# The last group of an experts' stage in a written order, its halves summed in the same banks; the embedding gate's start by token tiles

## The chip, the cores and the metric

The kernel runs on one core of a Trainium2 chip. The metric is the time of one execution in device microseconds (us). A core has a matmul engine (TensorE, PE in the profile, with its weight loads shown apart as PEld), VectorE (DVE), ScalarE (ACT), GpSimd (POOL), and a queue engine (SP), which issues nearly all of this kernel's transfers. Matmul results go to PSUM, a memory of eight banks; here they are two pools of four, "a" and "b".

## The reference

256 tokens of 1024 numbers (h) go through two layers and then a third block. Each layer is attention, then experts, then a gated embedding; the part that matters here, from the reference and cut:

```
h = h + mix                                                # attention
h = h + hier_moe(rms_norm(h, ln_ffn[i]), ...)              # experts
gate = jax.nn.sigmoid(rms_norm(h, ln_ple[i]) @ ple_w_gate[i])
h = h + gate * (p[i] @ ple_w_proj[i])                      # embedding gate

# hier_moe: 4 groups of 8 experts, each 1024 -> 128 -> 1024; a token takes one group and 2 experts of it
hid = silu(einsum('td,edf->tef', xt, w_gate)) * einsum('td,edf->tef', xt, w_up)
y = einsum('tef,efd->td', hid * cw[:, :, None], w_down)    # cw: weight of each token and expert
```

After the second layer comes a block with conditioning: a feed-forward part, a mixer, a second feed-forward part and a last norm, each preceded by a norm that is scaled and shifted. All is float32.

## The kernel before

**Layout.** h lies on chip as [128, 2, 1024]: two tiles of 128 tokens (t = 0, 1) by 1024 columns, cut into 8 pieces of 128 (kk, or k) and two halves of 512 (n, or ci). A float32 product is made of three faster ones: each operand is split into a high part, written by ACT, and a low part (the operand less its high part), written by DVE; mm3 then issues high x high (L306), high x low (L307) and low x high (L308). For weights this split is halves(): L293 on ACT, L294 on DVE, for a transfer of 1 MB in two parts (tiles raw to hi and lo).

**The experts' stage.** Function moe(i) runs once in each layer. For each of four groups (gq) tokens are gathered into slots, 32 for an expert, so that half a group (pp, four experts) fills 128 rows. A half goes through these steps:
- gate_up (L1056), four units u of two k each: the gathered tokens of an expert by its gate and up weights, plain float32; four experts lie side by side in 32 columns each of PE.
- the hidden tile, in finish(): Tanh on ACT (L1085), two steps on DVE (L1086, L1087), a transpose on PE (L1089), a copy on ACT (L1091).
- the down products (L1096): for each of the two column halves, four products of 32 columns side by side, one for each expert, into one bank of pool "a". One such group of four is called a set below. ACT scales the bank and writes its high part (L1099), DVE its low part (L1100), in tiles of the pool w4.
- token parts: two transposes (L1079) and a copy (GT, L1081) give the matrix that brings slots back to tokens.
- combine(): sums (L1109) of GT by high and low part into a bank, for each t and n, then an add on DVE to h (L486).

For groups 0 to 2, combine() sums both halves of a group in one bank and adds once. For the last group it runs for each half alone: finish(3, 0), combine, finish(3, 1), combine, each with four banks, eight sums and four adds. The down weights (wd) take their slots from the pools of hi and lo, four each.

**The embedding gate.** ple(i) follows. gained_T transposes h on PE (L373), 16 pieces of 128x128, and evacuates them by kk, both token tiles together (128x256): high part on ACT (L378), low part on DVE (L379). Then dense() multiplies by the gate's weights in two column parts of 512 (ci), 96 products in each; for the first part every weight piece is used for both token tiles at once, for the last part tile 0 runs through all weights and then tile 1. put() finishes each with Tanh, an embedding product that was made earlier, and an add to h (L1409 to L1411). The stage that follows begins with a norm's scale (rstd), the transposes of h by token tile (L419 transposes the scale) and, in the third block, modulated_T (L424 to L426).

**What sets the order.** Each engine runs its instructions in a fixed order that a scheduler works out when the kernel is built: each instruction has a priority by its place in the program, moved ahead by a fixed amount inside `with self.ahead_by(...)` (300 for "finish", 200 for "gain", 60 for "split"), and is placed when its operands and a free buffer are there by the scheduler's own estimate. Buffers go round in pools: raw 9, e 7, w4 5, hi and lo 4 each, GT 2, PSUM 4 and 4. DMAs are issued on SP as the raw tiles come free.

## Time and profile before

| what | us |
|---|---|
| median of 3 runs (1118.27 to 1119.1) | 1118.55 |
| the profiled execution | 1120.68 |
| its span in the trace | 1118.9 |
| end of the experts' stage, first layer | 289.16 to 324.64 |
| end of the experts' stage, second layer | 549.70 to 585.19 |
| gate of the second layer | 585.19 to 608.50 |
| start of the third block, to its first product | 608.50 to 617.04 |

The mean granted clock of TensorE over the profiled execution is 0.985. The profile is of one execution, about 2 us longer than the runs' median. Its numbers are of instructions on each engine: busy time, the mean duration of one, and the idle time before an instruction with what released it. Lines are those of the kernel before.

### The profile page before, as it was taken

What the parts mean: (1) busy time and instruction counts of PE and PEld (TensorE: products, weight loads), DVE (VectorE), ACT (ScalarE), POOL (GpSimd) and SP (SyncE); (2) the same over time, 40 slices, a digit from 0 to 9 for tenths busy, and PEclk for the clock granted to TensorE, in tenths of its full rate; (3) what the DMA queues carried; (4) which work ended last, traced back from release to release, by engine and by line L of the source; (5) the groups of instructions that cost most, each with busy time, mean ns of one, the idle gap of its engine ahead of it and who ended that gap; (6) DMA issues with size and microseconds to landing.
All of it is one profiled execution on the core that took longest, in us unless ns stands there. A gap on an engine that the chain in (4) does not pass through costs nothing.

```text
span 1118.9 us, 18106 instructions
## 1 busy us (share of the span) xinstructions
PE 1066.2 (95%) x6957; PEld 821.9 (73%) x6957; DVE 698.3 (62%) x1720; ACT 518.9 (46%) x1009; POOL 37.8 (3%) x43
## 2 busy tenths in 40 slices
PE   7999999999989999999989999999989989999996
PEld 6885557765547758666537799899969768999995
DVE  6686785644368965644358756575684866554555
ACT  5445585322257675222236544434454645444442
POOL 3000000200100000300000000000000000000000
PEclk9998999899999999999999999999999999999998
DMA  9656657599984477699795655845675354454310
GB/s 375 277 216 266 255 217 291 184 370 389 415 338 157 182 283 289 231 373 388 274 374 194 264 186 215 309 172 180 219 305 189 113 199 178 177 185 165 131 41 37
DMA packets 46506, 268.53 MB, mean 240 GB/s; under 512 B 5328, under 2 KB 7120, under 8 KB 20432
## 3 DMA queue, kind: packets, MB, share of 16 engines
q1 hardware_dynamic: 46416, 267.34, 63.4%
q8 instruction: 56, 0.92, 0.3%
q14 instruction: 34, 0.28, 0.1%
HBM read 266.27 MB, written 1.05 MB: 239 GB/s over the span
## 4 chain that ended last, share of the span: by engine, by line
PE 47%; DVE 3%; ACT 1%; issue 1%; DVEq 0%; ACTq 0%
PE b L306 7%; PE b L307 7%; PE b L308 7%; PE a L306 6%; PE a L308 6%; PE a L307 6%; PE a L1056 1%; DVE lo L294 1%; PE a L1096 1%; PE a L1450 1%; PE a L1109 1%; PE b L1466 1%; DVE w L1488 1%; DVE h L1489 0%; PE b L1035 0%
## 5 line engine op out<-in xcount | busy, mean ns | idle before, releaser
L294 DVE TENSOR_TENSOR lo<-raw,hi 128x1024 fp32r<-128x1024 f32 (+2 forms) x234 | 271.5, 1164 | 187.6 <-ACT hi L293 186.7
L293 ACT ACTIVATE hi<-raw 128x1024 fp32r<-128x1024 f32 (+2 forms) x234 | 234.6, 1008 | 247.5 <-PE b L307 125.5
L306 PE MATMUL a<-hi,e 128*128 128x512 f32 (+2 forms) x576 | 225.3, 392 | 1.8 <-ACT e L378 1.8
L307 PE MATMUL a<-lo,e 128*128 128x512 f32 (+2 forms) x576 | 223.7, 389 | 0.0
L308 PE MATMUL a<-hi,e 128*128 128x512 f32 (+2 forms) x576 | 222.8, 389 | 0.0
L306 PE MATMUL b<-e,hi 128*128 128x256 f32 x640 | 181.8, 284 | 0.0
L307 PE MATMUL b<-e,hi 128*128 128x256 f32 x640 | 181.4, 283 | 0.0
L308 PE MATMUL b<-e,lo 128*128 128x256 f32 x640 | 181.3, 283 | 0.0
L306 PEld LDWEIGHTS a<-hi,e 128*128 128x128 f32 x576 | 109.1, 190 | 25.0 <-ACT e L378 2.9
L308 PEld LDWEIGHTS a<-hi,e 128*128 128x128 f32 x576 | 108.8, 189 | 22.9 <-DVE e L379 1.1
L307 PEld LDWEIGHTS a<-lo,e 128*128 128x128 f32 x576 | 109.2, 190 | 21.5 <-DVE lo L294 1.2
L306 PEld LDWEIGHTS b<-e,hi 128*128 128x128 f32 x640 | 123.0, 192 | 1.1 <-ACT hi L293 0.8
L307 PEld LDWEIGHTS b<-e,hi 128*128 128x128 f32 x640 | 123.0, 192 | 0.3
L308 PEld LDWEIGHTS b<-e,lo 128*128 128x128 f32 x640 | 122.9, 192 | 0.0
L1056 PE MATMUL a<-raw,e 128*32 128x256 f32 x832 | 73.5, 383 | 1.1 <-DVEq L1293 0.8
L581 ACT ACTIVATE p<-p,m 128x128 f32<-128x128 f32 (+1 forms) x96 | 42.6, 448 | 8.9 <-DVE m L576 6.6
L486 DVE TENSOR_TENSOR h<-h,a 128x512 f32<-128x512 f32 x48 | 31.9, 685 | 21.7 <-PE a L1109 14.4
L1056 PEld LDWEIGHTS a<-raw,e 128*32 128x32 f32 x832 | 31.6, 110 | 18.6 <-issue 2.1
L1099 ACT ACTIVATE w<-a,sv 128x512 fp32r<-128x512 f32 x32 | 21.6, 687 | 46.6 <-PE a L1096 41.6
L1096 PE MATMUL a<-wd,hT 128*32 128x512 f32 x256 | 42.4, 600 | 0.0
L1035 PE MATMUL b<-G,e 128*128 128x256 f32 x256 | 38.9, 298 | 3.3 <-DVE ssv L351 2.0
L1109 PE MATMUL a<-w,GT 128*128 128x512 f32 x128 | 35.8, 412 | 6.2 <-ACT w L1099 5.1
(316 smaller groups left out, 1375.9 us busy)
## 6 DMA issues: line engine op xcount, KB each, us to landing
raw<-in_ffn SPq DMA_DIRECT2D x62, 1024.0 KB, 4.8
raw<-in_moe_gu SPq DMA_DIRECT2D x52, 1024.0 KB, 8.3
raw<-in_w_ada SPq DMA_DIRECT2D x36, 1024.0 KB, 5.1
wd<-in_moe_dn SPq DMA_DIRECT2D x64, 512.0 KB, 6.7
raw<-in_w_gate SPq DMA_DIRECT2D x8, 1024.0 KB, 11.2
raw<-in_w_m_in SPq DMA_DIRECT2D x8, 1024.0 KB, 4.9
raw<-in_w_a_in SPq DMA_DIRECT2D x7, 1024.0 KB, 10.9
e<-in_moe_gu SPq DMA_DIRECT2D x6, 1024.0 KB, 9.8
```

Of the source, the lines that this page charges most:

```text
L293: nc.scalar.activation(hi[:, sl], raw[:, at], AF.Copy)
L294: eng.tensor_tensor(lo[:, sl], raw[:, at], hi[:, sl], op=OP.subtract)
L306: mm(out, l[0], r[0], start=start, stop=False, **kw)
L307: mm(out, l[0], r[1], start=False, stop=False, **kw)
L308: mm(out, l[1], r[0], start=False, stop=stop, **kw)
L486: self.nc.vector.tensor_tensor(self.h[:, t, sl], self.h[:, t, sl], ps, op=OP.add)
L581: nc.scalar.activation(p, p, AF.Exp, bias=m[:, i:i + 1], scale=-1.0, accum_out=den[:, i:i + 1])
L1035: nc.tensor.matmul(ps[:, j], xh[part][:, t, sl], G[:, t], start=(t + j + part == 0), stop=(t + part == 2), skip_group_check=True)
L1056: nc.tensor.matmul(pgs[pp][32 * x:32 * x + 32], xg[:, k, o:o + 32], wg[kk][:, x], start=(k == 0), stop=(k == KT - 1))
L1096: nc.tensor.matmul(py[32 * x:32 * x + 32], hT[:, 32 * x:32 * x + 32], wd[2 * n + x // 2][:, x % 2], start=True, stop=True)
L1099: nc.scalar.activation(yh[:, sl], py, AF.Identity, scale=cw)
L1109: nc.tensor.matmul(ps, GT[:, t * P:(t + 1) * P], y[:, n * 512:(n + 1) * 512], start=(b == 0), stop=(b == len(back) - 1))
```

## The change

The last group of each experts' stage gets a function of its own, last_group(), whose instructions keep the order in which they are written (inline() stamps them on a line "tail" that the scheduler must follow). Group 2's combine moves into it. In it:
- both sets of a half are issued one after the other into pool "b", and only then their high and low parts are made (down_products);
- the sums of both halves of the last group go to the same four banks of pool "a" (start with the first product of the first half, stop with the last of the second), and h is added to once for each t and n, in the order of t;
- the token parts of both halves come after group 2's sums;
- the last group's second gate/up product takes its bank from pool "b";
- the split of the gate's first weight tile is called before the second hidden tile (gate_first, handed to dense()).

In K the head of ple goes from 0 to 1: gained_T evacuates by token tile (128x128 pieces, 16 on each engine, moved ahead by 200), and the first column part of the gate's products runs tile by tile too. The diff, cut to these parts:

```diff
-    head={'nsa': 0, 'ple': 0, 'moba': 0, 'mixer': 1},
+    head={'nsa': 0, 'ple': 1, 'moba': 0, 'mixer': 1},
...
+    def inline(self, ins, line="tail"):
+        self.tc.stamp_issue_order_token(ins.ins, line)
+        return ins
...
+        def down_products(gq, pp, wd, hT):
+            cw = st[gq][4][0][:, pp, 1:2]
+            with self.ahead_by("finish"):
+                yh, yl = self.w4([P, D], F32R), self.w4([P, D], F32R)
+                pys = []
+                for n in range(2):
+                    py = self.psb([P, 512])
+                    pys.append(py)
+                    for x in range(4):
+                        inline(nc.tensor.matmul(py[32 * x:32 * x + 32], hT[:, 32 * x:32 * x + 32],
+                                                wd[2 * n + x // 2][:, x % 2], start=True, stop=True))
+                for n, py in enumerate(pys):
+                    sl = slice(n * 512, (n + 1) * 512)
+                    inline(nc.scalar.activation(yh[:, sl], py, AF.Identity, scale=cw))
+                    inline(nc.vector.scalar_tensor_tensor(yl[:, sl], py, cw, yh[:, sl], op0=OP.mult, op1=OP.subtract))
+            return yh, yl
...
+        def last_group(back, values):
+            list(values)
+            first_hidden = hidden(3, 0)
+            next(first_hidden)
+            gate_up(3, 1, 0, None, self.psb)
+            gate_up(3, 1, 1)
+            hT = next(first_hidden)
+            combine_half(back, 0)
+            gate_up(3, 1, 2)
+            combine_half(back, 1)
+            GT = [token_parts(pp) for pp in range(2)]
+            gate_up(3, 1, 3)
+            y = [down_products(3, 0, wd[3, 0], hT)]
+            self.fine = bool(K["fine"])
+            self.gate_first = [list(self.halves(self.unit("w_gate", i * D * D, 2048), 2048, 4))]
+            second_hidden = hidden(3, 1)
+            next(second_hidden)
+            acc = [[self.psa([P, 512]) for _ in range(2)] for _ in range(2)]
+
+            def gathered(pp, n, t):
+                for part in range(2):
+                    inline(nc.tensor.matmul(acc[t][n], GT[pp][:, t * P:(t + 1) * P], y[pp][part][:, n * 512:(n + 1) * 512],
+                                            start=(pp + part == 0), stop=(pp + part == 2)))
+
+            with self.ahead_by("finish"):
+                for n in range(2):
+                    gathered(0, n, 0)
+                hT = next(second_hidden)
+                for n in range(2):
+                    gathered(0, n, 1)
+                y.append(down_products(3, 1, wd[3, 1], hT))
+                for t in range(2):
+                    for n in range(2):
+                        gathered(1, n, t)
+                        inline(self.add_h(n, t, acc[t][n]))
...
+            if gq == 3:
+                last_group(back, values)
+                break
...
+            if gq == 2:
+                continue
             combine(back)
```

hidden(), token_parts() and combine_half() hold the same instructions as finish() and combine() did, each stamped. In the order of the changed kernel the lines are others: gate_up L1062, hidden tile L1130 to L1138, down products L1151, parts L1155 and L1156, sums of the last group L1189, adds L492, splits L299 and L300.

The first place is PE near the end of the second layer's experts' stage: down products (w.. and hT to a bank), sums (GT) and, in the new order, the second hidden tile's transpose (hb). Before:

```order
L1096 MATMUL a_5993<-wd_5826,hT_5982 32x512 x2
L1109 MATMUL a_6000<-w4_5984,GT_5974 128x512
L1109 MATMUL a_6000<-w4_5985,GT_5974 128x512
L1109 MATMUL a_6004<-w4_5984,GT_5974 128x512
L1109 MATMUL a_6004<-w4_5985,GT_5974 128x512
L1096 MATMUL a_5993<-wd_5828,hT_5982 32x512 x2
L1109 MATMUL a_6008<-w4_5984,GT_5974 128x512
L1109 MATMUL a_6012<-w4_5984,GT_5974 128x512
L1096 MATMUL a_6031<-wd_5892,hT_6027 32x512 x2
L1109 MATMUL a_6008<-w4_5985,GT_5974 128x512
L1109 MATMUL a_6012<-w4_5985,GT_5974 128x512
L1096 MATMUL a_6031<-wd_5894,hT_6027 32x512 x2
```

And in the new order:

```order
L1136 MATMUL b_6037<-consts_88,hb_6025 128x128
L1189 MATMUL a_6031<-w4_5997,GT_5982 128x512
L1189 MATMUL a_6031<-w4_5998,GT_5982 128x512
L1189 MATMUL a_6032<-w4_5997,GT_5982 128x512
L1189 MATMUL a_6032<-w4_5998,GT_5982 128x512
L1151 MATMUL b_6047<-wd_5900,hT_6039 32x512 x2
L1151 MATMUL b_6047<-wd_5902,hT_6039 32x512 x2
L1151 MATMUL b_6052<-wd_5904,hT_6039 32x512 x2
L1151 MATMUL b_6052<-wd_5906,hT_6039 32x512 x2
L1189 MATMUL a_6029<-w4_6045,GT_5987 128x512
L1189 MATMUL a_6029<-w4_6046,GT_5987 128x512
L1189 MATMUL a_6030<-w4_6045,GT_5987 128x512
```

Before, the sets of a half come in pairs with sums between them, and the second half's sums have banks of their own; now the eight down products of a half stand together, and its sums go on in the banks of the first half (a_6029 to a_6032).

The second place is DVE from the last low part of the experts' stage into the gate (h the adds, e the gate's operands, raw its weights). Before:

```order
L1100 SCALAR_TENSOR_TENSOR w4_6030<-a_6038,sv_5951,w4_6029 128x512
L486 TENSOR_TENSOR h_87<-h_87,a_6053 128x512
L486 TENSOR_TENSOR h_87<-h_87,a_6057 128x512
L379 SCALAR_TENSOR_TENSOR e_6062<-b_6063,small_89,e_6061 128x256
L379 SCALAR_TENSOR_TENSOR e_6062<-b_6064,small_89,e_6061 128x256
L294 TENSOR_TENSOR lo_6131<-raw_6128,hi_6130 128x512 x2
L294 TENSOR_TENSOR lo_6149<-raw_6128,hi_6148 128x1024
L351 SCALAR_TENSOR_TENSOR ssv_6108<-ss_6099 128x2
```

And in the new order:

```order
L1156 SCALAR_TENSOR_TENSOR w4_6046<-b_6052,sv_5917,w4_6045 128x512
L492 TENSOR_TENSOR h_87<-h_87,a_6029 128x512
L492 TENSOR_TENSOR h_87<-h_87,a_6030 128x512
L492 TENSOR_TENSOR h_87<-h_87,a_6031 128x512
L492 TENSOR_TENSOR h_87<-h_87,a_6032 128x512
L396 SCALAR_TENSOR_TENSOR e_6074<-b_6075,small_89,e_6073 128x128
L396 SCALAR_TENSOR_TENSOR e_6074<-b_6076,small_89,e_6073 128x128
L300 TENSOR_TENSOR lo_6016<-raw_6013,hi_6015 128x512
```

All four adds now follow the last low part, where before two of them did; the evacuations are of 128x128 (sixteen in all, where eight of 128x256 stood; an order row stands for equal rows in a run), and the first weight split follows them.

The third place is DVE at the end of the second layer's gate and the start of the third block (raw_6446 and raw_6462 the feed-forward part's weights, w4 and h the gate's last steps, ssv the norm's scale). Before:

```order
L1410 SCALAR_TENSOR_TENSOR w4_6287<-w4_6287,e_4784 128x512
L1411 TENSOR_TENSOR h_87<-h_87,w4_6287 128x512
L294 TENSOR_TENSOR lo_6449<-raw_6446,hi_6448 128x1024
L420 COPY rbc_6311<-a_6310 128x128
L294 TENSOR_TENSOR lo_6459<-raw_6446,hi_6458 128x1024
L351 SCALAR_TENSOR_TENSOR ssv_6354<-squares_6202 128x1
L424 SCALAR_TENSOR_TENSOR xn_6322<-b_6308,mods_704,rbc_6311 128x128
L316 TENSOR_SCALAR nh_6357<-ssv_6354 128x1
```

And in the new order:

```order
L300 TENSOR_TENSOR lo_6465<-raw_6462,hi_6464 128x1024
L1511 SCALAR_TENSOR_TENSOR w4_6303<-w4_6303,e_4792 128x512
L300 TENSOR_TENSOR lo_6475<-raw_6462,hi_6474 128x1024
L1512 TENSOR_TENSOR h_87<-h_87,w4_6303 128x512
L300 TENSOR_TENSOR lo_6487<-raw_6484,hi_6486 128x1024
L426 COPY rbc_6327<-a_6326 128x128
L357 SCALAR_TENSOR_TENSOR ssv_6370<-squares_6194 128x1
L300 TENSOR_TENSOR lo_6497<-raw_6484,hi_6496 128x1024
L322 TENSOR_SCALAR nh_6373<-ssv_6370 128x1
```

A large weight split (128x1024) now stands between the gate's last two steps on DVE, where before they stood together. The orders on SP and POOL are the same in both kernels.

## Rows read from the trace of the kernel before

**Rows 1.** The page's first part: busy us (share of the span) and instructions.
```profile
PE 1066.2 (95%) x6957; PEld 821.9 (73%) x6957; DVE 698.3 (62%) x1720; ACT 518.9 (46%) x1009; POOL 37.8 (3%) x43
```

**Rows 2.** Windows: stretch, length, busy PE PEld DVE ACT POOL, clock, DMA, GB/s.
```profile
289.16:324.64 35.48, 30.67 (x239) 14.56 (x239) 15.62 (x31) 9.97 (x25) 1.89 (x2) 1.00 1.01 415
549.70:585.19 35.49, 30.68 (x240) 14.55 (x239) 15.63 (x31) 9.97 (x25) 0.00 (x0) 1.00 0.96 377
584.46:608.50 24.04, 23.50 (x102) 18.29 (x101) 19.22 (x45) 14.98 (x28) 0.00 (x0) 1.00 0.55 194
608.50:617.04 8.54, 5.79 (x52) 2.78 (x50) 7.59 (x23) 6.36 (x11) 0.00 (x0) 1.00 0.61 216
```

**Rows 3.** Chain of waits, second tail: start, length, engine, line and count.
```profile
568.75 1.01 PE a L1096 x8
569.78 0.69 ACT w L1099
570.50 0.76 DVE w L1100
...
572.27 1.01 PE a L1096 x4
```

**Rows 4.** PE's waits, 556.3 to 585.3: waiter, releaser, us in all, count, longest.
```profile
PE a L1109 <- ACT w L1099: 2.5, 4, 0.8
```

**Rows 5.** Timeline of PE and DVE, second tail: start, length, engine, line, operation.
```profile
547.12 1.93 PE L1096 MATMUL a<-wd,hT 128*32 128x512 f32 x16
...
556.39 1.05 PE L1096 MATMUL a<-wd,hT 128*32 128x512 f32 x4
...
560.15 3.49 PE L1109 MATMUL a<-w,GT 128*128 128x512 f32 x14
...
563.57 3.66 PE L1056 MATMUL a<-raw,e 128*32 128x256 f32 x64
...
583.17 1.28 DVE L486 TENSOR_TENSOR h<-h,a 128x512 f32<-128x512 f32 x2 [0.71 <-PE a L1109]
```

**Rows 6.** A window in the second gate.
```profile
598.00:608.00 10.00, 10.00 (x46) 8.29 (x45) 6.58 (x16) 4.25 (x9) 0.00 (x0) 1.00 0.51 188
```

**Rows 7.** Groups by form, 549.7 to 637.5: count, busy us, mean ns, idle before.
```profile
L425 ACT ACTIVATE e<-xn,mods 128x128 fp32r<-128x128 f32 x16 | 5.6, 391 | 4.9 <-DVE xn L424 4.9
L426 DVE SCALAR_TENSOR_TENSOR e<-xn,mods,e 128x128 fp32r<-128x128 f32 x16 | 5.2, 349 | 0.2 <-ACT e L425 0.2
...
L379 DVE SCALAR_TENSOR_TENSOR e<-b,small,e 128x256 fp32r<-128x256 f32 x8 | 3.7, 479 | 0.0
...
L1091 ACT ACTIVATE hT<-b 128x128 f32<-128x128 f32 x3 | 0.8, 268 | 0.0
...
L1087 DVE SCALAR_TENSOR_TENSOR hb<-hb,rr,a 128x128 f32<-128x128 f32 x2 | 0.7, 348 | 0.1
...
L1089 PE MATMUL b<-consts,hb 128*128 128x128 f32 x2 | 0.7, 328 | 1.1 <-DVE hb L1087 1.1
```

**Rows 8.** Timeline of DVE, second gate and the third block's start.
```profile
589.83 1.22 DVE L294 TENSOR_TENSOR lo<-raw,hi 128x1024 fp32r<-128x1024 f32 x1
...
618.10 0.93 DVE L426 SCALAR_TENSOR_TENSOR e<-xn,mods,e 128x128 fp32r<-128x128 f32 x3
```

**Rows 9.** DMA issues, 560.0 to 560.7 and 562.4 to 563.0: KB, us to landing.
```profile
raw<-in_w_gate SPq DMA_DIRECT2D x1, 1024.0 KB, 6.0
...
raw<-in_w_gate SPq DMA_DIRECT2D x1, 1024.0 KB, 12.8
```

**Rows 10.** PE's waits, 608.5 to 640.
```profile
PE a L419 <- DVE rstd L325: 2.8, 1, 2.8
```

**Rows 11.** Windows around the third block's start.
```profile
613.20:617.00 3.80, 1.05 (x11) 0.84 (x10) 3.80 (x18) 2.23 (x5) 0.00 (x0) 1.00 0.98 382
618.60:621.90 3.30, 3.30 (x9) 2.60 (x8) 3.30 (x9) 1.05 (x4) 0.00 (x0) 0.52 1.00 420
621.90:625.00 3.10, 3.10 (x15) 2.54 (x14) 1.23 (x5) 1.16 (x4) 0.00 (x0) 1.00 1.02 431
```

More of the change, by code (lines that the diff above doesn't have):

```diff
@@ L1045, in gather, with gate_up @@
                 gather_tile(gq, k, ps, t)
-        def gate_up(gq, pp, u, beside=None):
+        def gate_up(gq, pp, u, beside=None, bank=None):
             _, _, xg, pgs, _ = st[gq]
             if u == 0:
-                pgs.append(self.psa([P, 2, P]))
+                pgs.append((bank or self.psa)([P, 2, P]))
             where, wg = ahead.pop((gq, pp, u))
@@ L1055, in gate_up @@
                     o = pp * P + 32 * x
[L1056 to L1057 removed]
+                    mm = nc.tensor.matmul(pgs[pp][32 * x:32 * x + 32], xg[:, k, o:o + 32], wg[kk][:, x],
+                                          start=(k == 0), stop=(k == KT - 1))
+                    if gq == 3 and pp:
+                        inline(mm)
                     if beside and x % K["svx"] == 0:
@@ L1101, in finish, with token_parts @@
             return [(GT, yh), (GT, yl)]
+        inline = lambda ins: self.inline(ins, f"tail{i}")
+        def token_parts(pp):
+            G = st[3][0]
+            pv = self.psb([P, T])
+            for t in range(2):
+                inline(nc.tensor.transpose(pv[:, t * P:(t + 1) * P], G[:, t, pp * P:(pp + 1) * P].bitcast(F32),
+                                           self.ident))
+            GT = self.wk.tile([P, T], F32R, tag="GT", name="GT")
+            inline(nc.scalar.activation(GT, pv, AF.Copy))
+            return GT
@@ new lines, in hidden @@
+        def hidden(gq, pp):
+            pgs, (_, rr) = st[gq][3:]
+            pg = pgs[pp]
+            with self.ahead_by("finish"):
+                hb = self.wk.tile([P, P], F32, tag="hb", name="hb", bufs=1)
+                inline(nc.scalar.activation(hb, pg[:, 0], AF.Tanh, scale=rr[:, 0, pp:pp + 1]))
+                inline(nc.vector.scalar_tensor_tensor(hb, hb, 1.0, pg[:, 0], op0=OP.add, op1=OP.mult))
+                inline(nc.vector.scalar_tensor_tensor(hb, hb, rr[:, 1, pp:pp + 1], pg[:, 1], op0=OP.mult, op1=OP.mult))
+            yield
+            with self.ahead_by("finish"):
+                pt = self.psb([P, P])
+                inline(nc.tensor.transpose(pt, hb, self.ident))
+                hT = self.wk.tile([P, P], F32, tag="hT", name="hT", bufs=1)
+                inline(nc.scalar.activation(hT, pt, AF.Copy))
+            yield hT
@@ new lines, in down_products @@
+        def down_products(gq, pp, wd, hT):
+            cw = st[gq][4][0][:, pp, 1:2]
+            with self.ahead_by("finish"):
+                yh, yl = self.w4([P, D], F32R), self.w4([P, D], F32R)
[11 more added lines that the diff above has]
+            return yh, yl
@@ new lines, in combine_half @@
+        def combine_half(back, n):
+            for t in range(2):
+                ps = self.psa([P, 512])
+                for b, (GT, y) in enumerate(back):
+                    inline(nc.tensor.matmul(ps, GT[:, t * P:(t + 1) * P], y[:, n * 512:(n + 1) * 512],
+                                            start=(b == 0), stop=(b == len(back) - 1)))
+                inline(self.add_h(n, t, ps))
+        def last_group(back, values):
[20 more added lines that the diff above has]
+                                            start=(pp + part == 0), stop=(pp + part == 2)))
+            with self.ahead_by("finish"):
+                for n in range(2):
[4 more added lines that the diff above has]
+                y.append(down_products(3, 1, wd[3, 1], hT))
+                for t in range(2):
+                    for n in range(2):
+                        gathered(1, n, t)
+                        inline(self.add_h(n, t, acc[t][n]))
@@ L1225, in moe @@
             point(gq, 1)
-            if gq < 3:
-                slots_start(gq + 1)
-                slots(gq + 1)
-                for k in range(4):
-                    gather(gq + 1, k)
-            back = finish(gq, 0, wd[gq, 0])
-            if gq == 3:
-                combine(back)
-                back = []
-            else:
-                if not hold:
-                    load_down(gq + 1, 0)
-                for u in range(4):
-                    gate_up(gq + 1, 0, u)
+            slots_start(gq + 1)
+            slots(gq + 1)
+            for k in range(4):
+                gather(gq + 1, k)
+            back = finish(gq, 0, wd[gq, 0])
+            if not hold:
+                load_down(gq + 1, 0)
+            for u in range(4):
+                gate_up(gq + 1, 0, u)
             back = back + finish(gq, 1, wd[gq, 1])
             point(gq, 2)
-            if gq < 3 and not hold:
+            if not hold:
                 load_down(gq + 1, 1)
             point(gq, 3)
+            if gq == 2:
+                continue
             combine(back)
@@ L1413, in put @@
                 self.square_new(ci, t)
-        self.fine = bool(K["fine"])
-        self.dense(x, "w_gate", [512, 512], put, off=i * D * D, tail=True, head=K["head"]["ple"])
+        self.dense(x, "w_gate", [512, 512], put, off=i * D * D, tail=True, head=K["head"]["ple"], first=self.gate_first)
     def ada_start(self):
```

5 lines of the change are left out of this document (2 added, 3 removed).

## The prediction

> **What bounds the kernel now.** The page's first part comes first: PE is busy for 95% of the span [rows 1], so only time in which PE waits, or works in a slow form, can be won. Then the windows by stage: each experts' stage ends in a stretch of 35.5 us, from the first gate/up product of the last group to the first product of the embedding gate, in which PE is busy for only 30.7 us, at the full clock. The two stages agree to 0.01 us, so what is worked out for the second holds for the first too [rows 2]. The chain of waits in that stretch shows a round trip that comes back for every half of the down products: a set of products on PE, its high part on ACT (0.69 us), its low part on DVE (0.76), and only then the sums on PE [rows 3]. PE's own waits name the same place: 2.5 us in 4 waits for ACT's high part [rows 4]. There is also a loss that no wait shows. Four down products of 32 columns each run side by side: 16 records (8 products) take 1.93 us, so a set of four costs about 0.88 from start to start [rows 5]. Before issues several of them in pairs with other work between, and a pair (4 records) takes 1.01 us in the chain, like a whole set (8 records) [rows 3]. From 556.39 on the order has eight such slots where five sets would do: three too many.
>
> **The tail, step by step.** I start where both orders are alike, at the last set of group 2. Before is there at 556.39 [rows 5]; the two token transposes ahead of it (0.2 us) now come later, so 556.2. Durations [rows 5]: a set 0.88; eight sums 1.9 (14 span 3.49); a gate/up unit 0.87 (four span 3.66, of which 0.2 overlaps what follows); a change from 128-column to 32-column work 0.24 (563.57 less 560.15 less 14 x 0.227); an add 0.60 from start to start (two span 1.28). A product of the gate takes 0.227: 46 records touch 10 us, two of them in part [rows 6].
> - The set ends at 557.1. Two gate/up units (1.74) cover the hidden tile's steps on ACT and DVE, which are through at 558.2 as before; with its transpose, 559.0.
> - Eight sums, a change, a unit, eight sums, four token transposes (0.4), a change, a unit: 1.9 + 0.24 + 0.87 + 1.9 + 0.4 + 0.24 + 0.87 = 6.4, to 565.4. ACT and DVE have over 2 us for group 2's remaining parts, and its adds lie beside this.
> - Two whole sets: readable at 566.45 and 567.35. ACT 0.69 each, DVE 0.75 each: low parts at 567.95 and 568.85. The second hidden tile stands behind them on both engines: its Tanh (0.37) lies beside, then two steps of at most 0.35 on DVE, to 569.5 [rows 7].
> - Transpose 0.33 and copy 0.27 [rows 7]: 570.15. Beside it PE does the first half's sums, the last four after the transpose, to 570.6; a change: 570.8.
> - Two sets: readable at 571.85 and 572.75. ACT to 573.45, DVE to 574.2. The added wait is here: all four adds stand behind both low parts on DVE, and the transposes of h behind the adds. 3 x 0.60 + 0.68: h is whole at 576.7.
>
> Before has h whole at 584.45, the end of the two adds at 583.17 [rows 5]. The tail gives back 7.75 us.
>
> **The gate.** Before needs 24.05 us from there to the last product's end [rows 2]. In the new order DVE has, after the last add, sixteen evacuations of 128x128, two small and three large low parts. That evacuation does not stand in the gate before; the nearest rows are those of its size at the next stage's start, 0.39 on ACT and 0.35 on DVE for one [rows 7], and three on DVE span 0.93, so 0.28 or 0.29 each in a row [rows 8]. 16 x 0.28 + 2 x 0.60 + 2 x 1.17 + 1.22 = 9.3: the first two units' last low part is ready at about 586, against 591.05 before [rows 8]. Behind it the order has 64 of the 96 products, 14.5 us: the end is 600.7, again 24.0 us after h is whole. So I take the gate at no gain and no loss. DVE's extra 2.7 us (9.3 less 6.6) is hidden because 32 products are issued ahead of that split, where before had 19 (77 fit behind 591.05). Without that cover the gate costs up to 2.7 us more per stage. The early split of the first unit brings nothing: on ACT it stands behind the last high part.
>
> The rows show DVE at 0.48 us for one evacuation of 256 and 0.35 for one of 128 [rows 7]. The Trainium skill (Perfetto Trace Analysis, Optimizing Scalar/DVE Operations) says that each operation carries a fixed access cost, so that grouping helps a saturated engine, while smaller pieces may let work finish sooner where the engine is not saturated but holds up others. By its first half the gain would be 5.4 us smaller, by its second the sum stands. Which half applies no row settles: DVE is busy for 19.2 of the gate's 24.0 us [rows 2].
>
> **The rest.** Transfers: the order on SP is unchanged. The gate's weights land 6.0 us after the first issue at about 560.6 and 12.8 us after the last at about 562.5, so by 575.3 [rows 9]. They stand behind group 2's last down weights, whose slot now comes free some 3 us earlier, so I expect the last by about 572. The first is needed at 575.5, the second at 580: nothing is lost; without that cover each us late is a us lost.
> The next stage's start changes in the second stage only: PE waits there 2.8 us for the second half's scale [rows 10]. On DVE one large low part now stands between the last gate product's two steps, and the evacuations' first steps stand among the scale's chain. Stepped through, the first product starts 9.3 us after the gate's end instead of 8.54 [rows 2]: plus 0.8, with bounds of 0 (the chain waits for the square anyway) and 2.0.
> Other bounds, over both stages: sets that do not overlap (1.05 instead of 0.88, eight of them) plus 1.4; evacuations at 0.39 instead of 0.28 plus 3.5; the gate without cover plus 5.4; from below, a gate whose early products leave no stall (96 x 0.227 = 21.8 from 576.5, so 2.4 less each) minus 4.8. I take the values in the sum, those of the nearest rows.
>
> **Sum.** 2 x 7.75 = 15.5 off, 0.8 on: 14.7 us off. Against the profiled execution's own 1120.68 us (span 1118.9) that is 1106.0. The median of the runs, 1118.55, lies 2.1 lower, so I predict 1103.9 us. All later work only starts sooner.
>
> **Rivals.**
> - The gate loses what DVE has more. For: the last low part, not PE, sets when the dense run begins. Against: 32 products are there to fill. Plus 5.4 to 6 us: 1109.6.
> - A larger gain, the gate without a stall: for, PE can start it at 576.5; against, DVE's 9.3 us. 1099.
> - Slower: the clock falls in the new tail. At a granted 0.52, the lower level (1.2 GHz), PE did 9 products in 3.3 us, and 15 in 3.1 at the upper one; it had fallen after 3.8 us in which PE was busy for 1.05 [rows 11]. Between 565.4 and 586 the new order has 48 products and four sets with pauses between; at the lower level they cost 48 x 0.20 + 4 x 0.88 = 13.1 us more per stage. This decides once more than 7.4 of the 13.1 are lost, that is with the clock low for over half of that stretch; low throughout it is 1118.55 - 14.7 + 26.2 = 1130. Against: before has pauses of the same kind in its tail, at 1.00 throughout [rows 2].
> - It does not do what it says: the gate's products of both token tiles stand interleaved, not tile by tile; if the sums wait for banks as well, nothing is won: 1118.
> The Trainium skill (Perfetto Trace Analysis, Matmuls) wants independent groups to rotate through the banks, so that one is read beside the next group's products. Here four banks are held until the last half is in, and the adds stand bare, 2.5 us instead of 1.3; that is in the steps above already.
>
> **Numbers.** The forecast (1101 to 1107) 0.58; the smaller gain (1107 to 1116) 0.24; the larger 0.10; no change 0.03; slower 0.05. The range 1099 to 1111.5 leaves out the last two and the far ends of the second and third, under 2 in 10. A change of 0.2% (2.2 us) is about the least that can be told from none here. Faster 0.92, same 0.03, slower 0.05.
>
> **What would show it.** Right: the stretch to the first gate product near 27 us instead of 35.5 in both stages; the last group's down products in four slots; four adds in a row right before the transposes of h; the gate's end 23 to 25 us after the last add; clock 1.00. Wrong: PE waiting for a PSUM bank or a down weight in the tail, a gate of 27 us, a granted clock near 0.5 before the dense run, or a next stage that starts over 10.5 us after the gate.

## The result

The changed kernel takes 1105.86 us (median of 4, 1103.13 to 1108.57) against 1118.82 before; the ratio is 0.9878, with a 95% interval of 0.985 to 0.9906. Forecast were 1103.9 us and a range of 1099 to 1111.5. Timed once more beside the first experiments it is 1105.21 (6 runs) against 1119.36, ratio 0.9868 [0.9848, 0.9888].

Its ten executions lie in two groups, 1102.2 to 1103.4 and 1107.1 to 1108.6, and the mean granted clock goes with them: 0.988 to 0.990 in the first, 0.983 to 0.985 in the second. So kernels are compared below in two ways that do not hang on this: by the length of a stage in the trace, and by the span times its mean granted clock, an estimate of the span at the full clock. (It takes half of all time at the lower level away, also where PE had to wait anyway.) This span times clock is 1103.1 before (mean of 11 runs) and 1088.2 after (10 runs, 1086.9 to 1089.5): 14.9 us less, where the sum said 14.7.

PE's share of the shorter span is higher than in [rows 1]:

```profile
PE 1059.7 (96%) x6957; PEld 822.8 (74%) x6957; DVE 695.8 (63%) x1728; ACT 522.7 (47%) x1025; POOL 37.8 (3%) x43
```

The windows of the changed kernel answer to [rows 2]: from the last group's first gate/up product to the gate's first product in both layers, the second gate, and the third block's start.

```profile
290.00:317.08 27.08, 26.09 (x235) 14.08 (x235) 12.46 (x25) 8.50 (x20) 1.90 (x2) 1.00 1.02 414
545.22:572.28 27.06, 26.07 (x235) 14.07 (x235) 12.44 (x25) 8.49 (x20) 0.00 (x0) 1.00 0.97 374
572.21:596.79 24.58, 23.26 (x104) 18.30 (x103) 20.11 (x51) 18.14 (x39) 0.00 (x0) 1.00 0.79 313
596.79:606.00 9.21, 5.83 (x52) 2.82 (x50) 9.12 (x27) 5.71 (x10) 0.00 (x0) 1.00 0.63 209
```

PE was idle for 4.8 us of the tail before and is for 1.0 now, at the full clock in both; PE's busy time in the tail falls as well, from 30.7 to 26.1 us, with the same number of down products and sums. Before, PE had these waits beside the 2.5 us of [rows 4]:

```profile
PE b L1089 <- DVE hb L1087: 1.1, 2, 0.8
PE a L1109 <- DVE w L1100: 0.6, 2, 0.3
PE b L373 <- DVE h L486: 0.5, 1, 0.5
```

Now these are left:

```profile
PE a L1189 <- DVE w L1156: 0.6, 2, 0.3
PE b L1136 <- DVE hb L1132: 0.2, 1, 0.2
```

The timeline of PE and DVE there shows what took the place of [rows 3, 5]: eight products (16 records) in 1.90 us, the first half's sums around the hidden tile's transpose, eight products again, and four adds in a row.

```profile
560.95 1.90 PE L1151 MATMUL b<-wd,hT 128*32 128x512 f32 x16
...
563.58 1.36 PE L1189 MATMUL a<-w,GT 128*128 128x512 f32 x3 [0.28 <-DVE w L1156]
565.11 0.30 PE L1136 MATMUL b<-consts,hb 128*128 128x128 f32 x1 [0.16 <-DVE hb L1132]
565.17 1.17 PE L1189 MATMUL a<-w,GT 128*128 128x512 f32 x4
566.27 1.92 PE L1151 MATMUL b<-wd,hT 128*32 128x512 f32 x16
...
569.65 2.56 DVE L492 TENSOR_TENSOR h<-h,a 128x512 f32<-128x512 f32 x4
```

Three lengths are used from here on. The tail runs from the last group's first gate/up product to the end of the last add to h, the gate from there to the first transpose of the next stage, the start from there to the third block's first product. All in us, from each kernel's trace; where a stage stands twice, both layers. The runs were made in three batches, in which the median of before was 1119.36 (changed, own banks, pairs, hidden tile early), 1120.28 (no fixed order, both kernels of the tail, gate by tiles alone) and 1120.05 (the rest). Its span times clock was 1103.1, 1102.7 and 1103.1 in them, so differences of some 0.5 us in that column tell nothing.

| kernel | tail | gate | start | span x clock (runs) | median |
|---|---|---|---|---|---|
| before | 34.74, 34.75 | 24.04, 24.04 | 8.54 | 1103.1 (11) | 1119.36 |
| changed | 27.00, 26.99 | 24.58, 24.58 | 9.21 | 1088.2 (10) | 1105.21 |
| own banks | 26.99, 26.99 | 24.60, 24.58 | 9.17 | 1088.3 (4) | 1105.07 |
| pairs | 29.91, 29.91 | 24.57, 24.57 | 9.18 | 1094.3 (4) | 1113.29 |
| no fixed order | 34.80, 34.80 | 27.64, 27.73 | 8.42 | 1107.7 (4) | 1128.08 |
| tail alone | 27.00, 27.00 | 28.76, 29.79 | 10.23 | 1092.6 (5) | 1114.48 |
| tail, whole evacuations first | 27.00, 27.00 | 24.62, 24.62 | 8.81 | 1087.8 (4) | 1102.51 |
| gate by tiles alone | 34.86, 34.88 | 27.22, 26.74 | 8.17 | 1104.3 (10) | 1123.89 |
| the same, PE kept busy | 34.88, 34.88 | 25.80, 25.75 | 8.17 | 1105.8 (10) | 1121.83 |
| hidden tile early | 24.94, 24.94 | 24.05, 24.06 | 9.50 | 1085.2 (5) | 1104.21 |
| add first | 26.99, 27.00 | 24.57, 24.57 | 8.18 | 1088.3 (4) | 1102.53 |
| both of these | 24.94, 24.95 | 24.03, 24.07 | 8.44 | 1085.1 (5) | 1099.50 |

### The profile page after: what moved, and what is told of

Same layout as the page of the kernel before. It is cut to its first block, busy times and chain, and to the rows that moved or that the text cites. A ratio compares the mean times of both kernels' runs of the same rounds, so it can differ in the third digit from the quotient of the medians.

```text
span 1106.8 us, 18131 instructions
## 1 busy us (share of the span) xinstructions
PE 1059.7 (96%) x6957; PEld 822.8 (74%) x6957; DVE 695.8 (63%) x1728; ACT 522.7 (47%) x1025; POOL 37.8 (3%) x43
## 4 chain that ended last, share of the span: by engine, by line
PE 47%; DVE 3%; ACT 1%; issue 1%; DVEq 0%
PE b L312 7%; PE b L313 7%; PE b L314 7%; PE a L312 6%; PE a L313 6%; PE a L314 6%; PE a L1062 1%; DVE lo L300 1%; PE a L1550 1%; PE b L1566 1%; DVE w L1588 1%; DVE h L1589 0%; PE a L1104 0%; PE b L1041 0%; PE a L1163 0%
## 5 line engine op out<-in xcount | busy, mean ns | idle before, releaser
L300 DVE TENSOR_TENSOR lo<-raw,hi 128x1024 fp32r<-128x1024 f32 (+2 forms) x234 | 271.6, 1163 | 188.7 <-ACT hi L299 185.6
L299 ACT ACTIVATE hi<-raw 128x1024 fp32r<-128x1024 f32 (+2 forms) x234 | 235.7, 1011 | 249.4 <-PE b L313 125.5
L1062 PE MATMUL a<-raw,e 128*32 128x256 f32 x704 | 66.2, 383 | 1.1 <-DVEq L1394 0.8
L1041 PEld LDWEIGHTS b<-G,e 128*128 128x128 f32 x256 | 34.0, 197 | 8.4 <-issue 6.3
L1062 PEld LDWEIGHTS a<-raw,e 128*32 128x32 f32 x704 | 27.5, 109 | 15.6 <-issue 2.1
L335 ACT ACTIVATE junk<-h 128x512 bf16<-128x512 f32 x40 | 25.4, 643 | 25.4 <-DVE h L1589 10.7
L492 DVE TENSOR_TENSOR h<-h,a 128x512 f32<-128x512 f32 x40 | 26.7, 684 | 15.9 <-PE a L1163 6.6
L1550 PE MATMUL a<-raw,c 128*32 128x512 f32 x224 | 35.9, 654 | 0.0
```

Of the source, the lines that this page charges most:

```text
L299: nc.scalar.activation(hi[:, sl], raw[:, at], AF.Copy)
L300: eng.tensor_tensor(lo[:, sl], raw[:, at], hi[:, sl], op=OP.subtract)
L335: self.nc.scalar.activation(junk, self.h[:, t, half * 512:(half + 1) * 512], AF.Square, accum_out=out)
L492: return self.nc.vector.tensor_tensor(self.h[:, t, sl], self.h[:, t, sl], ps, op=OP.add)
L1041: nc.tensor.matmul(ps[:, j], xh[part][:, t, sl], G[:, t], start=(t + j + part == 0), stop=(t + part == 2), skip_group_check=True)
L1062: mm = nc.tensor.matmul(pgs[pp][32 * x:32 * x + 32], xg[:, k, o:o + 32], wg[kk][:, x], start=(k == 0), stop=(k == KT - 1))
```

## The experiments

**The changed kernel again.** No edit.

> The changed kernel itself once more. Its four times so far lie at two levels, 1103.2 and 1108.5 us, with a mean granted clock of 0.988 and 0.983. Theory: the two levels differ in the number of low-clock stretches (at 1.2 GHz) alone, of which the trace at 1108.5 shows five of 3.4 us and two of 6.8 us, one more than the trace of before (at 524.6 to 528.0, after a pause of 2.6 us in the overflow step); a stretch of 3.4 us costs 1.7 us, so a trace at the lower level shows some three of them fewer, and the stretches from the tail to the gate's end are as long as in the first trace (27.0 us from the last group's set to the gate's dense end less than 0.3 us apart). Rival: the levels come from the tail or the gate, by a transfer that lands late in some executions; then those stretches differ by up to 2.7 us a stage between the traces.

The profiled run fell in the upper group again (1107.45, clock 0.983), so no trace of the changed kernel itself shows the lower one; its tail and gate are as in the first trace (27.00 and 24.63, 26.99 and 24.60). The next experiment's trace, with the same stages at 1101.07 us, shows what differs. One of the places is the step before the second tail: PE waits 2.61 us for DVE in both. Then the same four products of 128x512 take 3.48 us in the changed kernel and 1.98 in the other. Timeline of the changed kernel, and the window of those products (in the columns of [rows 2]):

```profile
524.38 3.48 PE L1466 MATMUL a<-w,hTo 128*128 128x512 f32 x4 [2.61 <-DVE hTo L1461]
```

```profile
524.00:527.40 3.40, 3.02 (x4) 1.48 (x5) 1.07 (x2) 0.00 (x0) 0.00 (x0) 0.50 0.82 333
```

The same two views of the other:

```profile
521.25 1.98 PE L1465 MATMUL a<-w,hTo 128*128 128x512 f32 x4 [2.61 <-DVE hTo L1460]
```

```profile
521.80:525.20 3.40, 3.15 (x8) 1.12 (x6) 2.47 (x4) 0.00 (x0) 0.00 (x0) 1.00 0.88 358
```

Over the whole run the trace at 1101.07 has 17.1 us at 1.2 GHz (its end left out), the changed kernel's 30.7, four stretches of 3.4 us more. Half of the difference, an estimate of its cost, is 6.8 us, and the times differ by 7.5. The theory holds, though it is shown on this neighbour and not on two traces of one kernel. The Trainium skill (TensorE: Matmul & The Clock Gate, Part 1) says that the chip sets this rate by how busy PE has lately been, and that its phase against the kernel is not the same from run to run. The two traces agree with that: behind the same pause of 2.61 us the clock is at 0.50 in one and at 1.00 in the other.

**Own banks.** Each half is summed in banks of its own and added by itself:

```diff
+                ps = self.psa([P, 512])
                 for part in range(2):
-                    inline(nc.tensor.matmul(acc[t][n], ..., start=(pp + part == 0), stop=(pp + part == 2)))
+                    inline(nc.tensor.matmul(ps, ..., start=(part == 0), stop=(part == 1)))
+                inline(self.add_h(n, t, ps))
```

> The two halves of the last group no longer share their sums' banks: each half has four banks of its own in turn and is added to h by itself (eight adds in place of four), in the same fixed order otherwise. Theory (the gain is the fixed order and the whole sets of down products; sharing banks saves adds only where DVE waits anyway): tail and total as in the changed kernel, plus 0 to 0.5 us a stage, total within 1 us at the same clock. Rival (the shared banks carry the gain, since four adds and the banks' release leave the path): plus 2.4 us a stage, total plus 5 us.

The tail is 26.99 us, no longer than in the changed kernel, and span times clock 1088.3. Sharing the banks gains nothing. The four more adds lie where DVE waits: ahead of the second half's low parts it is idle for 0.77 us here and for 3.16 in the changed kernel.

**Pairs.** One sum goes behind each pair of the second half's down products:

```diff
                         inline(nc.tensor.matmul(py[32 * x:32 * x + 32], hT[...], wd[...], start=True, stop=True))
+                        if turns and x % 2:
+                            turns.pop(0)()
```

> The second half's eight down products no longer stand together: they are issued in four pairs, with one sum of the first half behind each pair (the four sums that stood ahead of them). Theory (a pair between other work costs like a whole set of four, 0.98 to 1.0 us): four slots of 1.0 and four sums of 0.23 are 4.9 us where 1.17 + 1.88 = 3.05 stood, so h is whole 1.9 to 2.5 us later in each stage, total plus 3.8 to 5 us. Rival (products cost the same wherever they stand, 0.22 each): plus 0 to 0.4 us a stage, total plus 0 to 0.8.

The tail is 2.92 us longer in each layer, somewhat more than the theory's price, and span times clock 6.1 us higher (1094.3). PE's timeline shows why:

```profile
566.13 1.05 PE L1151 MATMUL b<-wd,hT 128*32 128x512 f32 x4 [0.43 <-ACT hT L1138]
567.11 0.50 PE L1198 MATMUL a<-w,GT 128*128 128x512 f32 x1
567.54 1.05 PE L1151 MATMUL b<-wd,hT 128*32 128x512 f32 x4
568.52 0.50 PE L1198 MATMUL a<-w,GT 128*128 128x512 f32 x1
```

A pair is followed by the next work 0.98 us after its start, as a set would be, and the single sum holds the place for 0.43 where it takes 0.23 among its like. Another 0.43 us of the 2.92 is PE's wait for the hidden tile, which the four sums covered where they stood before. The Trainium skill (TensorEngine Tiling, Key Properties) says that a change of the tiling mode drains the engine. These rows agree in that each sum between pairs holds PE for 0.20 us more; what PE does in that time no row shows.

**Hidden tile early.** The second hidden tile's steps go ahead of the first half's parts, and the sums go by column half:

```diff
+                if step:
+                    next(step)              # Tanh and two DVE steps of the second hidden tile
                 for n, py in enumerate(pys):
+                    if step and n:
+                        hidden_T.append(next(step))     # its transpose and copy
...
+                y.append(down_products(3, 1, wd[3, 1], hidden_T[0]))
+                for n in range(2):
+                    for t in range(2):
+                        gathered(0, n, t)
+                    for t in range(2):
+                        gathered(1, n, t)
+                        inline(self.add_h(n, t, acc[t][n]))
```

> The second hidden tile's steps on ACT and DVE go ahead of the first half's high and low parts, its transpose and copy right behind the first half's down products, and the second half's products follow at once; the sums then go by column half (first half's two, second half's two, an add after each of these), for both column halves. Theory (in the changed kernel the second hidden tile stands behind the first half's parts on ACT and DVE and so sets the tail's end): from the first half's last set on PE has 1.9 us of products and 16 sums (3.7) without a wait, h is whole 2.0 to 2.5 us earlier in each stage, total 4 to 5 us less than the changed kernel at the same clock. Rival (the gate is bound by DVE's own chain or by the weights' landing, so an earlier h only makes the gate longer): h earlier, the gate's end not; total within 1 us.

The tail is 2.05 us shorter in both layers, as expected, and the gate 0.5 shorter too. In the tail PE now waits once:

```profile
556.97 1.90 PE L1153 MATMUL b<-wd,hT 128*32 128x512 f32 x16
558.80 0.33 PE L1138 MATMUL b<-consts,hb 128*128 128x128 f32 x1
559.50 1.92 PE L1153 MATMUL b<-wd,hT 128*32 128x512 f32 x16 [0.37 <-ACT hT L1140]
561.35 3.97 PE L1194 MATMUL a<-w,GT 128*128 128x512 f32 x16
```

Of the 5.1 us that the two layers give, 3.0 arrive at the end (1085.2), where the theory had 4 to 5. One place of loss is seen: at the start of the stage behind the first layer's gate PE waits 0.7 us for the gate's last add, ahead of which DVE has a weight split.

**Gate by tiles alone.** The kernel before with one setting:

```diff
-    head={'nsa': 0, 'ple': 0, 'moba': 0, 'mixer': 1},
+    head={'nsa': 0, 'ple': 1, 'moba': 0, 'mixer': 1},
```

> The kernel before with one setting changed: the embedding gate begins by token tiles (head ple 1), the experts' stage as before. Theory (the gain is the tail's; the gate's start by tiles neither gains nor costs much, since DVE and ACT have sixteen evacuations where eight stood, and the first products need less): from h whole to the gate's end 24.0 to 24.6 us where 24.04 stood, the third block's start 0 to 0.8 longer, total 0 to 2 us above before. Rival (the start by tiles carries a part of the gain): the gate 1 us or more shorter in each stage, total 2 us or more below before.

Neither came: it is slower, ratio 1.0037 [1.0023, 1.005], with gates of 27.22 and 26.74 us. Windows around the second gate's first product (590.03) show PE without work for 2 us, and then half the clock:

```profile
588.00:590.03 2.03, 0.00 (x1) 0.01 (x1) 1.86 (x7) 2.03 (x7) 0.00 (x0) 1.00 0.23 85
590.30:593.70 3.40, 2.94 (x7) 1.81 (x7) 3.40 (x8) 3.40 (x7) 0.00 (x0) 0.50 0.07 10
```

PE's wait there names the high part of a weight on ACT (589.32 to 589.97). Ahead of it ACT has three squares of h, nine evacuations and another weight split:

```profile
PE a L306 <- ACT hi L293: 2.1, 1, 2.1
```

**The same, PE kept busy.** Twenty more transposes of h, into a bank that nothing reads, behind those that the gate needs:

```diff
+                    spare = self.psa([P, 512])
+                    for n in range(20):
+                        mm = nc.tensor.transpose(spare[:, n % 4 * P:n % 4 * P + P], ..., self.ident)
```

> The kernel before with the gate begun by token tiles, as in the run of that setting alone, and twenty more transposes of h on PE right behind those that the gate needs (into a spare bank that nothing reads); the order of everything else is the same. In the run without them PE did nothing from 587.9 to 590.0 us, the granted clock was 0.5 from 590.3 to 593.7 (in the first stage from 327.4 to 330.9), and the gate took 27.2 and 26.7 us from h whole where 24.04 stood. Theory (of these 2.7 to 3.2 us some 1.7 are the clock, which fell because PE paused, and 1.0 to 1.5 are the order on ACT and DVE): with PE busy through the pause the clock stays at 1.00 at the gate's start in both stages, the gate takes 25.0 to 25.6 us, total 2.5 to 3.5 us below the run without them, though PE has 4.4 us more work. Rival (the clock's fall does not come from the pause, or costs nothing where PE waits anyway): the gate 26.7 to 27.5 us, total the same or up to 4 us above.

The clock stays at 1.00 at both gates' starts, and they take 25.80 and 25.75, 1.4 and 1.0 us less. So the low clock cost that, a little less than the 1.7 expected. The other 1.7 us over 24.04 are put down to the order on ACT and DVE; no run of the kernel before changes that order alone. The median is 2.1 us lower though PE has 4 us more work, with ratios of 1.0037 and 1.0024 [1.0012, 1.0036] to before, whose intervals overlap: the gates of the two traces show the gain, the time does not quite. The mean clock goes with it, 0.981 to 0.985 in the ten runs without the extra work and 0.987 to 0.988 in eight of the ten with it. (Span times clock rises, from 1104.3 to 1105.8: since it takes the cost of the low clock away, it cannot show what holding the clock up gains.) The window with the extra work, and the one behind it:

```profile
587.50:589.50 2.00, 2.00 (x20) 1.87 (x18) 1.83 (x6) 2.00 (x7) 0.00 (x0) 1.00 0.31 127
589.50:592.90 3.40, 2.63 (x11) 1.90 (x11) 3.32 (x9) 3.40 (x8) 0.00 (x0) 1.00 0.01 5
```

**The tail alone.** The changed kernel with head ple 0 again and without the early call of the first split:

```diff
-    head={'nsa': 0, 'ple': 1, 'moba': 0, 'mixer': 1},
+    head={'nsa': 0, 'ple': 0, 'moba': 0, 'mixer': 1},
...
-            self.gate_first = [list(self.halves(self.unit("w_gate", i * D * D, 2048), 2048, 4))]
```

> The changed kernel with the gate's start as before (head ple 0) and without the early call of the first weight split: the tail alone. Its tail is as in the changed kernel (20.66 us from the last value product of the stage to h whole in both). For the gate the order on DVE has five weight splits ahead of the evacuations of 128x256, which before stood behind them. Theory (what DVE does first after the last add sets the gate's start): the first low part of h comes 5 us after the last add, PE then has 21.8 us of products, the gate takes 26 to 27.2 us in place of 24.58, total 3 to 5.5 us above the changed kernel at the same clock. Rival (the gate is bound by its last weights' low parts whatever stands first): 24.0 to 24.6, total within 1 us.

The tail is 27.00, the gate 28.76 and 29.79, still longer than the theory had it: PE's one wait in the second gate is 4.2 us for the first evacuation on ACT, which stands behind five weight splits and four squares. Span times clock (1092.6) is 4.4 us above the changed kernel, inside the theory's range. The traced execution is the slowest of five (1120.68, the others 1112.55 to 1115.03), so the gates of the others may be shorter.

```profile
PE a L312 <- ACT e L384: 4.2, 1, 4.2
```

From the last part of that wait on the clock is low:

```profile
581.30:588.20 6.90, 5.98 (x14) 4.36 (x15) 5.78 (x23) 4.01 (x10) 0.00 (x0) 0.51 1.02 419
```

**Whole evacuations first.** The tail alone, with the evacuations of 128x256 moved ahead by 200:

```diff
+                    with self.ahead_by("gain") if first else nullcontext():
                         self.last = nc.scalar.activation(hi[:, kk], p, AF.Identity, scale=g[:, kk:kk + 1])
                         nc.vector.scalar_tensor_tensor(lo[:, kk], p, g[:, kk:kk + 1], hi[:, kk], op0=OP.mult, op1=OP.subtract)
```

> As the tail alone, but the eight evacuations of 128x256 are moved ahead by as much as the changed kernel's sixteen of 128x128 are, so that they stand first on DVE and ACT behind one small weight split. Theory (evacuations of half the size let products start in the order in which they are needed; eight large ones in a row keep the second weight piece's low part back to 5.0 us after the last add, with six products issued until then): the gate takes 25 to 25.8 us, 0.4 to 1.2 a stage more than in the changed kernel, total plus 1 to 2.5. Rival (DVE's work is what counts: eight of 0.48 are 2.7 us a stage less than sixteen of 0.28 with their splits): the gate 0.5 to 2.5 us shorter than 24.58, total minus 1 to 5.

Neither: the gate takes 24.62, as with sixteen pieces (24.58). PE waits elsewhere, 1.67 us for the second weight's low part, and gets through the rest without a pause. So the gate's start by token tiles is worth nothing by itself. That evacuations stand ahead of the weight splits is worth 4 to 5 us a layer between these two traces, the clock included, and 2.4 without it, by span times clock (1092.6 against 1087.8).

**No fixed order.** The stamp is left out:

```diff
     def inline(self, ins, line="tail"):
-        self.tc.stamp_issue_order_token(ins.ins, line)
         return ins
```

> The changed kernel without the fixed order: the same functions, but the scheduler places their instructions. It puts the second hidden tile ahead of the first half's parts and lets the adds of h begin between the last low parts, but issues the second half's down products in four pairs with sums between. Theory (whole sets are what the fixed order wins; a pair costs a set's time): 20.66 us from the last value product to h whole becomes 21.5 to 23 us, total 2 to 5 us above the changed kernel at the same clock, and still some 10 below before. Rival (the fixed order wins nothing beyond the new functions): within 0.5 us a stage, total within 1.

Both were wrong by far: the tail is 34.80, as long as before, the gate 27.7 (with the clock at 0.5 for 3.4 us behind pauses of PE, in both layers), and the kernel slower than before, ratio 1.007 [1.0051, 1.0088]. PE's timeline in the second tail has the down products in seven slots of about 1 us, and the round trip over ACT once more between them:

```profile
574.68 0.50 PE L1188 MATMUL a<-w,GT 128*128 128x512 f32 x1 [0.81 <-ACT w L1154]
575.11 1.04 PE L1150 MATMUL b<-wd,hT 128*32 128x512 f32 x2
...
578.67 0.98 PE L1188 MATMUL a<-w,GT 128*128 128x512 f32 x3 [1.03 <-ACT w L1154]
579.57 1.05 PE L1150 MATMUL b<-wd,hT 128*32 128x512 f32 x4
...
583.29 0.73 PE L1188 MATMUL a<-w,GT 128*128 128x512 f32 x2 [0.79 <-ACT w L1154]
583.95 1.05 PE L1150 MATMUL b<-wd,hT 128*32 128x512 f32 x4
```

**Add first.** The changed kernel with the second of the next block's weight splits on DVE held behind the gate's last add (second layer):

```diff
+            if ci and t and (0, 2)[i]:
+                self.inline(add, f"put{i}")
+                self.behind = [f"put{i}", (0, 2)[i]]     # halves() stamps that split on the same line
```

> The changed kernel with one weight split on DVE held behind the gate's last add to h in the second stage (in the changed kernel that split of 1.2 us stands between the gate's last product step and its last add). Theory (that split is what makes the third block's start longer: 9.2 us where before took 8.5): the last add ends 1.1 us earlier, the norm's scale too, from the gate's end to the block's first product 8.0 to 8.6 us, total 0.6 to 1.2 less at the same clock. Rival (the scale waits for ACT's sum of squares or another split, so nothing moves): 9.2 again. What would eat the gain: the splits that come later now have to be made while the products run.

The start falls from 9.21 to 8.18, so the split was its cause. On DVE the add now follows the step before it, where in the changed kernel a split stood between them. The changed kernel's DVE, then this run's:

```profile
598.42 0.69 DVE L1511 SCALAR_TENSOR_TENSOR w<-w,e 128x512 f32<-128x512 f32 x1
599.02 1.22 DVE L300 TENSOR_TENSOR lo<-raw,hi 128x1024 fp32r<-128x1024 f32 x1
600.16 0.68 DVE L1512 TENSOR_TENSOR h<-h,w 128x512 f32<-128x512 f32 x1
...
594.84 0.69 DVE L1517 SCALAR_TENSOR_TENSOR w<-w,e 128x512 f32<-128x512 f32 x1
595.56 0.69 DVE L1518 TENSOR_TENSOR h<-h,w 128x512 f32<-128x512 f32 x1
596.17 1.22 DVE L301 TENSOR_TENSOR lo<-raw,hi 128x1024 fp32r<-128x1024 f32 x1
```

But little or nothing is left of it at the end (1088.3 against 1088.2). Between equal products of the two traces, with the low clock taken out, the lead is 1.0 us at the block's first product, 0.5 some fifteen us later and 0.2 some thirty us later. With the clock left in it is 1.9 us there, since the changed kernel is at 0.50 from 605.9 to 609.3 and this one at 1.00 in the block's start. In the next kernel, whose start is 8.44, the clock falls there again (596.8 to 600.2), so it is not shown that a shorter start keeps it up.

**Both of these.** The early hidden tile, and a split held behind the last add in both layers (the fourth in the first).

```diff
-            if ci and t and (0, 2)[i]:
+            if ci and t and (4, 2)[i]:
```

> The two that should add up: the second hidden tile ahead of the first half's parts with the sums by column half (3.0 us below the changed kernel as span times granted clock, 1085.2 against 1088.2), and one weight split held behind the gate's last add, in both stages (in the first stage of that kernel a split of 1.2 us stands between the last two steps as well, and PE then waits 0.7 us for that add). Theory: 1.0 to 1.4 us less at the first stage's end and 0.6 to 1.2 at the second's, so 1083.0 to 1083.6 as span times clock, 4.5 to 5 below the changed kernel. Rival (what follows waits for something else): 1085 again.

Span times clock is 1085.1, no lower than with the early hidden tile alone, so the rival has it for the held split. Its five runs (1098.60 to 1100.74) are all faster than every run of the changed kernel: median 1099.50, ratio to before 0.9819 [0.9806, 0.9833]. The lower median beside the early tile's 1104.21 comes with a clock of 0.988 to 0.990; the held split is not shown to have any part in it.

## Why the prediction was right, and where not

- **The tail: right to 0.01 us.** 7.75 a layer were forecast, 7.74 and 7.76 came. The steps hold one by one, counted from the same set: h whole at 572.21, where the forecast's 576.7 less the 4.5 us that this trace is ahead there gives 572.2. Whole sets in a fixed order, the cause that it gave, are shown by two runs: with pairs the second half alone gives 2.92 back, without the order all goes. The round trip between the sets, which it named beside them, was not changed by itself. The shared banks, which the sum did not count as a gain, are none. The second hidden tile behind the parts, which the steps had on the path, costs 2.05 (with the order of the sums).
- **The gate: taken as no loss, 0.54 a layer in fact.** The time for DVE was right: its last low part ends at 581.61, 9.4 us after h is whole, where 9.3 was the sum, and the 32 products ahead of it did cover that. No wait of PE in the tail or the gate names a transfer, as forecast. What the sum left out are PE's waits ahead of that split, above all one for ACT, which got sixteen evacuations as well: 0.33 and 0.99 us, where before had one of 0.52 (timelines, before first):

```profile
587.63 0.51 PE L306 MATMUL a<-hi,e 128*128 128x512 f32 x1 [0.52 <-ACT e L378]
...
573.53 0.50 PE L313 MATMUL a<-lo,e 128*128 128x512 f32 x1 [0.33 <-DVE lo L300]
...
577.80 0.50 PE L312 MATMUL a<-hi,e 128*128 128x512 f32 x1 [0.99 <-ACT e L395]
...
580.39 1.22 DVE L300 TENSOR_TENSOR lo<-raw,hi 128x1024 fp32r<-128x1024 f32 x1
```

  With the early tile one wait of 0.69 is left, for ACT, and the gate takes 24.05; no run changes ACT's evacuations alone. The rule of the Trainium skill that the prediction weighed (Perfetto Trace Analysis, Optimizing Scalar/DVE Operations) decides nothing here: eight large evacuations and sixteen small ones give the same gate.
- **The price without cover** was set at 2.7 us. Put into the kernel before, the gate by tiles costs 3.2 and 2.7; but 1.0 to 1.4 of that are the clock, which that bound did not hold, so that without it the price was 1.7.
- **The third block's start: 0.67 longer where 0.8 was forecast**, for the reason named. But the run with the add first shows that little or none of this lasts to the end.
- **The early split brings nothing**, as forecast: in the kernel without that call the order on PE, ACT and DVE is the same row for row, which leaves nothing to time.
- **The sum** at equal clock is thus 14.7 forecast, 14.9 measured, with a gate term 1.1 too low and a start term up to 0.8 too high, and some 0.5 us that no stage here accounts for, which is as much as span times clock differs between batches. So it is luck that the sum comes within 0.2: its tail is right, and its two errors lie in opposite directions. The forecast also took over from before how much longer the traced execution is than the median. The median is 2 us above the forecast since half of the runs have more time at the low clock, and with two runs in each group of the first four it could as well have come out near 1103 or 1108. The rival of a slower kernel put the clock's fall into the new tail; no trace has it there. (Its price of 0.20 us a product holds: in the tail alone the gate's products start 0.42 to 0.43 us apart at the low clock, from 584.30 on, where 0.227 is usual.) In the stages looked at here it falls in the step before the second tail in some executions, at the gate's start in kernels whose gate begins with longer pauses (waits of 2.1, 2.9 and 4.2 us in the second gates), and at the third block's start in some traces, that of before among them ([rows 11]).
- What stays open: what the round trip alone cost, why the executions of one kernel differ in where the clock falls, and where 2 of the 5 us of the early hidden tile go.

## What to carry to other kernels

Where products in small column groups run side by side, issue all that fit together as one piece and fix that order: here the scheduler, left to place them by readiness, split them, and each pair cost as much as a whole set. Look at what ACT and DVE do first after the value that everything waits for: work that could be done later and stands ahead there cost more (4 to 5 us a layer between two traces, 2.4 without the clock) than the choice of the evacuations' size, which made no difference. When a median lies between two groups of runs, compare stages in the traces before explaining it.

## What was not expected of the hardware

A pause of PE at the start of a dense run cost more here than its length: behind 2.0 us without work the clock was 0.50 for 3.4 us, and with twenty useless transposes in that pause it stayed at 1.00 and the gates were 1.0 to 1.4 us shorter (one trace of each kernel, both layers). A pause of 2.61 us at another place was followed by the low clock in one trace and not in the other.
